# Grouped off-diagonal products, two late tile loads, and the merge weights' split on VectorE in a hybrid decoder layer

## The chip, the cores and the metric

The kernel runs on one core of one Trainium2 chip. Its time is the device time of a launch in microseconds (us). A core has TensorE (PE: matrix products, with PEld for its weight loads), VectorE (DVE), ScalarE (ACT), GpSimd (POOL) and SyncE (SP, which issues most DMAs). A profile is one execution taken by the hardware profiler; its clock column is the granted clock of TensorE, 1.00 for 2.4 GHz.

## The reference

One layer of a hybrid decoder, for a prompt of 1024 tokens (with 16 learned ones ahead of it) and 8 samples of 8 tokens, in float32 with 1024 model columns:

```
h = h + 1/2 * post1(SwiGLU_1(pre1(h)))                       # FFN 1, 2816 wide
u = pre_mix(h) @ w_in     # q|k|v (short conv), gate z, beta, decay, window q|k|v, two merge gates
A: gated DeltaNet, 8 heads of 128, chunks of 64, gated RMSNorm
B: attention over a window of 128 past tokens, 8 heads, sinks, ALiBi, 16 meta keys
y = sigmoid(gate_A) * o_A + sigmoid(gate_B) * o_B
h = h + post_mix(y @ w_out)                                  # the merge
h = h + 1/2 * post2(SwiGLU_2(pre2(h)))                       # FFN 2
```

Branch A, per head and chunk of 64 tokens:

```
a_mat = where(strict, beta * (k @ k.T) * decay, 0) + eye     # 64 x 64, lower triangular
u, w  = solve(a_mat, [v * beta | k * beta * exp(gc)])
step:  u' = u - w @ S;  o = (q * exp(gc)) @ S + (q @ k.T * decay) @ u'
       S  = S * c_decay + k_dec.T @ u'
```

Outputs are y for prompt and samples and the new states.

## The kernel before

Every large product is made from three products of parts: an operand is split into a high part (cast to a shorter format, names ending in h) and the rest (l), and hh + lh + hl is summed; L128, L130 and L132 are these three. FFN 1 runs first, then the projections and the window (branch B), then the eight heads of branch A, then the merge, then FFN 2. The order on PE is the order in which the program issues (manual); the instructions of the other engines are ordered by a scheduler, except where they are pinned to program order. `weave` interleaves several streams of work: each is given a begin and an end as shares of the whole, and a number of steps.

The heads (`heads`, 1273 to 1832 us). The 16 prompt tiles of 64 tokens are taken as eight chunks of 128 a head, in two halves g of four. A chunk needs the inverse R of its 128 x 128 triangular matrix: the two 64 x 64 diagonal inverses come by DMA (L1490), and the block off the diagonal is their product round a block bo. `prep` of a half makes it in two steps: L1502 multiplies bo by rt on the 64 x 64 tile of the array at (0, 64), ACT copies it out as xt (L1504), L1516 multiplies xt by R at (64, 0), and ACT copies the result into R (L1518). All use one PSUM buffer, tag "tr", as do the transposes for vs (L1510, scaled by ACT in L1512), the squares (L1539, ACT L1541, names sqp and cq) and the product of kf and q (L1527, DVE L1529, pm). `chain` carries the state S through the chunks: L1641, then DVE b (L1643), L1651 with R, ACT xs (L1653), L1656 and L1662, then DVE S (L1658) and o (L1664), ACT sq (L1602), DVE f (L1604), POOL f (L1606), ACT on (L1607). `emit` turns the outputs (L1689), multiplies them into the gate Z (L1691), adds the window's part yw (POOL, L1696) and stores y (L1697). Beside the chain of a head run the gate projection z of that head, the conv projections of the next, and the early part of the next head's preparation (`prep8`, then `prep` of the first half). Beside the gate of the last head `load_w` reads w_out, casts it (ACT, L1774) and subtracts (POOL, L1775) to get the low part, in 16 pieces of 128 x 512.

The merge (`run`, 1815 to 1945 us) takes nine tiles of tokens in the order 0, 4, 1, 5, 2, 8, 6, 3, 7. `load` of a tile reads y (L1877), casts its high part yh on ACT (L1791) and subtracts the low part yl on DVE (L1792). `tile_` makes 48 products a tile into two halves "dn", which ACT evacuates (L1900; L1897 for the short tile 8). `finish` norms it and adds the residual (L81, POOL L660, L82, L83, DVE L659, L90). `feed` turns an earlier tile (L207) and makes the operands of FFN 2 from it: ACT x10h to x70h (L213), DVE x10l to x70l (L214) and sums (L262 on DVE and POOL). Before, the load of the next tile is always issued ahead of the present tile's products.

Of the kernel before, what the change touches and what calls it, by code (L numbers as in the profile page):

```python
# [34 lines left out]
def f32(ap):  # L35
    return ap.bitcast(F32)
# [698 lines left out]
class Mixer:  # L735
# [733 lines left out]
    def persistent(self, pool):  # L1469
        c, nc = self.c, self.nc  # L1470
        self.ms = [c.t(pool, [P, 8, P], tag=f"ms{i}") for i in range(1)]
        self.p8 = [c.t(pool, [80, P], tag=f"p8{i}") for i in range(2)]
        self.on8 = c.t(pool, [P, 1, P], tag="on8")
        for m in (*self.ms, *self.p8, self.on8):
            nc.gpsimd.memset(m, 0.0)

    def prep(self, h, g, pool):

        c, nc = self.c, self.nc
        T = lambda shape, tag, bufs=None, dt=F32: c.t(pool, shape, dt, tag=tag, bufs=bufs)  # L1480
        x = self.hd[h]
        ts = range(4 * g, 4 * g + 4)
        cols = slice(4 * g * P, (4 * g + 4) * P)
        R = x["R", g] = T([P, 4, P], f"R{g}")
        rt = T([64, 4, 64], "rt", 2)
        bo = T([64, 4, 64], "bo", 2)
        nc.gpsimd.memset(R[64:P, :, 0:64], 0.0)
        for half in range(2):
            r = slice(half * 64, half * 64 + 64)
            nc.sync.dma_start(R[r, :, r], self.lr_d[h, ts.start:ts.stop, half].rearrange("t r c -> r t c"))  # L1490
        nc.sync.dma_start(rt, self.lrt_d[h, ts.start:ts.stop, 0].rearrange("t r c -> r t c"))
        nc.sync.dma_start(bo, self.bo_d[h][:, ts.start:ts.stop])
        kf = x["kf", g] = T([P, 4, P], f"kf{g}")
        nc.sync.dma_start(kf, self.kf_d[h][:, cols].rearrange("p (t k) -> p t k", k=P))
        pm = x["pm", g] = T([P, 4, P], f"pm{g}")
        nc.sync.dma_start(pm, self.dt_d[h][:, ts.start:ts.stop, :])
        kd = x["kd", g] = T([P, 4, P], f"kd{g}")
        nc.sync.dma_start(kd, self.kd_d[h][:, ts.start:ts.stop, :])

        px = self.ps([P, 4, P], "tr")  # L1500
        for t in range(4):
            nc.tensor.matmul(px[64:P, t, 0:64], bo[:, t, :], rt[:, t, :], start=True, stop=True, tile_position=(0, 64))  # L1502
        xt = T([P, 4, 64], "xt")
        nc.scalar.copy(xt[64:P], px[64:P, :, 0:64])  # L1504
        yield

        vs = x["vs", g] = T([P, 4, P], f"vs{g}")
        pt = self.ps([P, 4, P], "tr")
        for i, t in enumerate(ts):
            nc.tensor.transpose(pt[:, i, :], x["cv"][:, t * P:(t + 1) * P], self.k(C_IDENT))  # L1510
        for i, t in enumerate(ts):
            nc.scalar.activation(vs[:, i, :], pt[:, i, :], AF.Copy, scale=self.nr[:, h, t:t + 1])  # L1512
        yield
        px = self.ps([P, 4, P], "tr")
        for t in range(4):
            nc.tensor.matmul(px[0:64, t, 0:64], xt[64:P, t, :], R[64:P, t, 64:P], start=True, stop=True,  # L1516
                             tile_position=(64, 0))
        nc.scalar.copy(R[0:64, :, 64:P], px[0:64, :, 0:64])  # L1518
        yield

        cq = x["cq", g] = T([P, 4], f"cq{g}")
        self.squares(h, cq, [x["qv"][:, t * P:(t + 1) * P] for t in ts], pool)
        yield

        pk = self.ps([P, 4, P], "tr")
        for i, t in enumerate(ts):
            nc.tensor.matmul(pk[:, i, :], kf[:, i, :], x["qv"][:, t * P:(t + 1) * P], start=True, stop=True)  # L1527
        for i, t in enumerate(ts):
            nc.vector.scalar_tensor_tensor(out=pm[:, i, :], in0=pk[:, i, :], scalar=self.s[:, h, t:t + 1],  # L1529
                                           in1=pm[:, i, :], op0=ALU.mult, op1=ALU.mult)  # L1530
        yield
# [149 lines left out]
    def emit(self, h, pool):  # L1681

        nc = self.nc
        x = self.hd[h]
        Z = x["Z"]
        for on, t0, n, w in x["on"]:
            pt = self.ps([P, 4, P], "on")
            for i in range(n):
                nc.tensor.transpose(pt[:, i, :], on[:, i, :], self.k(C_IDENT))  # L1689
            zc = Z[:, t0 * P:t0 * P + n * w].rearrange("p (i w) -> p i w", w=w)  # L1690
            nc.vector.scalar_tensor_tensor(out=zc, in0=pt[:, :n, P - w:], scalar=self.nw, in1=zc, op0=ALU.mult,  # L1691
                                           op1=ALU.mult)
            cols = slice(t0 * P, t0 * P + n * w)
            yw = self.c.t(pool, [P, 512], tag="yw", bufs=1)
            nc.sync.dma_start(yw[:, :n * w], self.yw_d[h][:, cols])
            nc.gpsimd.tensor_tensor(out=Z[:, cols], in0=Z[:, cols], in1=yw[:, :n * w], op=ALU.add)  # L1696
            nc.sync.dma_start(self.y_d[t0][h], Z[:, cols])  # L1697
            yield

    def heads(self, pool, mg):  # L1700
        def early(h):
            yield from self.prep8(h, pool)
            yield from self.prep(h, 0, pool)

        def early0():
            prep = self.prep(0, 0, pool)
            yield from steps_of(prep, 1)
            yield from steps_of(prep8, 1)
            self.solves8(pool)
            yield from prep  # L1710
            yield from prep8

        z0 = self.z_gate(0, pool)
        prep8 = self.prep8(0, pool)
        weave((steps_of(z0, 72), 0, 1, 72), (early0(), 0.7, 1, 8))
        for h in range(H):
            streams = [(self.chain(h, pool), 0, 1, 29), (self.prep(h, 1, pool), 0, 0.35, 5)]
            if h:
                streams += [(self.emit(h - 1, pool), 0, 0.2, 3)]
            if h < H - 1:  # L1720
                if h:
                    streams += [(self.qv_steps(h + 1, pool), 0, 0.5, 145), (self.z_gate(h, pool), 0.5, 1, 145)]
                else:
                    streams += [(self.qv_steps(1, pool), 0, 0.55, 145), (z0, 0.55, 1, 73)]
                streams += [(early(h + 1), 0.75 if h else 0.8, 1, 8)]
            else:
                out = self.emit(h, pool)
                streams += [(self.z_gate(H - 1, pool, mg.load_w), 0, 0.95, 145), (steps_of(out, 2), 0.6, 1.15, 2)]
                begin = mg.begin()
                streams += [(steps_of(begin, 1), 0.6, 0.6, 1)]  # L1730
            weave(*streams)
        weave((begin, 0, 1, 42), (out, 0.1, 0.2, 1), (self.left, 0.15, 0.5, 4))
        drain(mg.begin_last(self.hd[H - 1]["Z"][:, 0:P]))
# [15 lines left out]
class Merge:  # L1749
# [8 lines left out]
    def load_w(self, i):  # L1758

        c, nc = self.c, self.nc  # L1760
        parts = new_chunk(c, self.xp[i], i)
        ks = ((2, 3, 4, 5), (6, 7), (0, 1))[i]
        flat, loaded = [x.rearrange("p k t -> p (k t)") for x in parts], []
        for j, k in enumerate(ks):
            wh, wl = (x[:, j * D:(j + 1) * D] for x in flat)
            raw = f32(c.t(self.m.wraw, [P, KD, P], F32R, tag="raw")).rearrange("p k f -> p (k f)")
            nc.sync.dma_start(raw, self.I["w_out"][:, k, :])
            self.w[k] = wh, wl
            loaded.append((raw, wh, wl))
        yield  # L1770
        for raw, wh, wl in loaded:
            for q in range(2):
                cols = slice(q * D // 2, (q + 1) * D // 2)
                c.tc.keep_in_program_order(nc.scalar.copy(wh[:, cols], raw[:, cols]))  # L1774
                nc.gpsimd.tensor_tensor(out=wl[:, cols], in0=raw[:, cols], in1=f32(wh[:, cols]), op=ALU.subtract)  # L1775
                yield

    def pair(self, yh, yl):
# [88 lines left out]
        yield from right(pool, self.f2.ptr, x8, y8, 8)  # L1867
        yield from right(pool, self.f2.ptr, self.o[3], self.o[7], 7)

    def load(self, t):  # L1870
        c, nc, pool = self.c, self.nc, self.pool
        n = min(TILES[t][1], 1088 - TILES[t][0])
        yl = c.t(pool, [P, H, P], F32R, tag="yl")
# [2 lines left out]
        for ks in (slice(0, H - 1), slice(H - 1, H)) if t == 4 else (slice(0, H),):  # L1876
            nc.sync.dma_start(f32(yl)[:, ks, :n], y[ks, :, t % 4 * P:t % 4 * P + n].rearrange("h p t -> p h t"))  # L1877
            if n == 64:
                self.pair(yh, yl)
            else:  # L1880
                self.split(yh, yl, ks, n)
        return yh, yl, n

    def tile_(self, t, yh, yl, n, o):
# [22 lines left out]
    def run(self, f2, es):  # L1907
# [9 lines left out]
        for i in range(1, 9):  # L1917
            if i == 5:
                f2.ahead(self.pool, "yl")
            now, y = y, self.load(order[i + 1]) if i < 8 else None  # L1920
            done = []
            if i > 1 and order[i - 2] != 6:

                done = [(self.feed(order[i - 2]), *((0.05, 0.45) if order[i - 2] in (4, 5) else (0.6, 0.95)), 2)]
            o = c.t(*((self.first, [P, H, P], F32R, "yh") if i % 3 == 0 else (self.pool, [P, H, P], F32R, "o")))
            weave((self.tile_(order[i], *now, f32(o).rearrange("p h t -> p (h t)")), 0, 1, 33 if order[i] == 8 else 49), *done)
        pso.close()


# [308 lines left out]
```

## Time and profile before

| | before |
|---|---|
| median of 3 runs | 2669.57 us (2669.01 to 2672.76) |
| profiled execution | 2665.62 us, span 2663.8 |
| mean granted clock | 0.992 |
| PE busy | 2593.7 us, 97% |
| DVE, ACT, POOL busy | 59%, 42%, 48% |
| chain that ended last | PE 47% |

Busy shares are means over stages with different limits: PE is full for most of the span, while the other engines have room, and only few stretches show PE idle. A wait in brackets behind a row of the timeline is idle time of that engine ahead of the row, with what ended it.

### The profile page before, as it was taken

To read this page: it belongs to the slowest core of one execution; us is meant where nothing else is said; L and a number is where in the kernel's file an instruction comes from. 1 tells how busy PE (TensorE), PEld (TensorE's weight loads), DVE (VectorE), ACT (ScalarE), POOL (GpSimd) and SP (SyncE) were. 2 spreads that over 40 slices of the span, in tenths; PEclk is the share of its full clock that TensorE was granted. 3 is DMA by queue.
4 is the path that set the end of the run, shared out by engine and by line. 5 is a ranking of instruction groups with operands and counts; after the bars stand their busy time and mean duration, and the time that the engine had idled before them with its cause. 6 is when DMAs were issued, how large, how long until landed. Compare 5 with 4: busy or idle time off the path is not lost.

```text
span 2663.8 us, 49377 instructions
## 1 busy us (share of the span) xinstructions
PE 2593.7 (97%) x18993; PEld 2475.1 (93%) x18993; DVE 1558.4 (59%) x2315; ACT 1130.7 (42%) x2728; POOL 1268.4 (48%) x1205
## 2 busy tenths in 40 slices
PE   7999999999999999999999999999899999999998
PEld 7999999999988999888889999997699999999998
DVE  7657565545677726995454444444466656554566
ACT  6333343432145634457444444454443434334221
POOL 6656555445524533433343333435565555554471
PEclk9999999999999999999999999999999999999999
DMA  4344343667544744335333333335443434338764
GB/s 164 121 152 152 127 167 117 242 227 253 190 151 151 230 148 130 106 122 176 98 106 88 89 95 99 100 93 160 138 132 140 167 127 149 127 137 319 244 225 145
DMA packets 231570, 406.48 MB, mean 153 GB/s; under 512 B 61814, under 2 KB 123414, under 8 KB 231046
## 3 DMA queue, kind: packets, MB, share of 16 engines
q1 hardware_dynamic: 211030, 324.75, 38.0%
q10 hardware_dynamic: 20304, 78.56, 7.5%
q8 instruction: 150, 2.46, 0.4%
q14 instruction: 86, 0.70, 0.1%
HBM read 264.36 MB, written 140.53 MB: 152 GB/s over the span
## 4 chain that ended last, share of the span: by engine, by line
PE 47%; DVE 1%; ACT 1%; POOL 1%; issue 1%; DMA 0%; POOLq 0%; DVEq 0%; SPq 0%; ACTq 0%
PE y L532 9%; PE B L352 7%; PE C L352 5%; PE A L352 4%; PE gu L132 4%; PE gu L128 4%; PE gu L130 4%; PE dn L128 1%; PE dn L132 1%; PE dn L130 1%; PE ch L1651 1%; PE tr L1527 1%; PE ch L1656 0%; PE oq L1646 0%; PE on L1673 0%
## 5 line engine op out<-in xcount | busy, mean ns | idle before, releaser
L132 PE MATMUL gu<-xh,wl 128*128 128x512 f32 (+3 forms) x1456 | 495.7, 340 | 0.0
L128 PE MATMUL gu<-xh,wh 128*128 128x512 f32 (+3 forms) x1456 | 491.9, 338 | 0.0
L130 PE MATMUL gu<-xl,wh 128*128 128x512 f32 (+3 forms) x1456 | 490.6, 337 | 0.0
L318 POOL TENSOR_TENSOR wl<-T,wh 128x512 fp32r<-128x512 f32 x246 | 330.5, 1350 | 314.1 <-ACT wh L317 244.4
L532 PE MATMUL y<-hb,wh 128*128 128x256 f32 (+2 forms) x2528 | 430.6, 290 | 2.1 <-ACT acc L572 1.0
L318 POOL TENSOR_TENSOR wl<-raw,wh 128x512 fp32r<-128x512 f32 x200 | 282.9, 1423 | 249.0 <-ACT wh L317 191.1
L532 PEld LDWEIGHTS y<-hb,wh 128*128 128x128 f32 x2528 | 366.1, 189 | 3.2 <-ACT acc L572 1.2
L317 ACT CAST wh<-T 128x512 fp32r<-128x512 f32 x246 | 152.2, 620 | 362.5 <-PE B L352 110.4
L132 PEld LDWEIGHTS gu<-xh,wl 128*128 128x128 f32 x1456 | 276.9, 190 | 16.4 <-issue 0.4
L130 PEld LDWEIGHTS gu<-xl,wh 128*128 128x128 f32 x1456 | 276.9, 190 | 16.3 <-issue 0.4
L128 PEld LDWEIGHTS gu<-xh,wh 128*128 128x128 f32 x1456 | 276.7, 190 | 16.4 <-issue 0.9
L532 PE MATMUL y<-hb,wl 128*128 128x256 f32 (+2 forms) x1264 | 271.8, 289 | 0.0
L317 ACT CAST wh<-raw 128x512 fp32r<-128x512 f32 x200 | 122.4, 621 | 276.8 <-PE C L352 81.9
L806 POOL TENSOR_TENSOR wl<-raw,wh 128x1024 fp32r<-128x1024 f32 x58 | 141.0, 2431 | 180.6 <-ACT wh L805 161.5
L543 DVE TENSOR_TENSOR acc<-acc,y 128x552 f32<-128x552 f32 (+4 forms) x216 | 144.9, 679 | 139.0 <-PE y L532 138.7
L532 PEld LDWEIGHTS y<-hb,wl 128*128 128x128 f32 x1264 | 207.1, 188 | 0.0
L292 DVE TENSOR_TENSOR T<-raw,raw 128x512 f32<-128x512 f32 x124 | 117.0, 948 | 107.1 <-POOL wl L318 107.1
L1606 POOL TENSOR_TENSOR f<-f,mhalf 128x1 f32<-128x1 f32 (+1 forms) x72 | 54.8, 762 | 125.5 <-DVE f L1604 119.2
L303 DVE TENSOR_TENSOR T<-raw,T 128x512 f32<-128x512 f32 x62 | 65.5, 1059 | 61.8 <-POOL wl L318 61.4
L292 DVE TENSOR_TENSOR T<-raw,T 128x512 f32<-128x512 f32 x62 | 63.3, 1028 | 31.9 <-POOL wl L318 31.5
L966 DVE SCALAR_TENSOR_TENSOR cv<-pc,cw,cv 128x1131 f32<-128x1131 f32 x48 | 66.8, 1393 | 21.4 <-POOL cv L963 20.8
L1111 DVE TENSOR_TENSOR ltmp<-la 72x14 f32<-72x14 f32 (+37 forms) x76 | 72.1, 948 | 12.3 <-DMA la<-b_d 11.4
(612 smaller groups left out, 7298.1 us busy)
## 6 DMA issues: line engine op xcount, KB each, us to landing
hb<-hid SPq DMA_DIRECT2D x71, 552.0 KB
hb<-hid SPq DMA_DIRECT2D x71, 544.0 KB
hid<-hs ACTq DMA_DIRECT2D x69, 552.0 KB
hid<-hs ACTq DMA_DIRECT2D x69, 544.0 KB
raw<-in_w_in_dram SPq DMA_DIRECT2D x58, 512.0 KB
raw<-in_ffn_w_gate_dram SPq DMA_DIRECT2D x100, 256.0 KB
raw<-in_ffn_w_up_dram SPq DMA_DIRECT2D x94, 256.0 KB
raw<-in_ffn_w_down_dram SPq DMA_DIRECT2D x88, 256.0 KB
```

The source lines that it names most:

```text
L128: nc.tensor.matmul(ps, wh, xh, start=first and i == 0, stop=False)
L130: nc.tensor.matmul(ps, wh, xl, start=False, stop=False)
L132: nc.tensor.matmul(ps, wl, xh, start=False, stop=last and i == n - 1)
L292: pin(self.nc.vector.tensor_tensor(out=b[name], in0=b[x], in1=b[y], op=ALU.subtract))
L317: self.nc.scalar.copy(hi, s)
L318: self.nc.gpsimd.tensor_tensor(out=lo, in0=s, in1=f32(hi), op=ALU.subtract)
L352: self.nc.tensor.matmul(self.view(ps, (i,)), w[a][:, k * P:(k + 1) * P], self.X[p][i][b][:, k, :], start=first and k + a + b == 0, stop=k ...
L532: self.nc.tensor.matmul(self.view(ps[d], (i,)), w[x][:, d * P:(d + 1) * P], hb[:, y, lo:hi], start=j + x + y == 0, stop=j == len(items) - ...
L543: dve = lambda out, x, y: nc.vector.tensor_tensor(out=out, in0=x, in1=y, op=ALU.add)
L806: low.tensor_tensor(out=lo, in0=raw, in1=f32(hi), op=ALU.subtract)
L966: nc.vector.scalar_tensor_tensor(out=cv, in0=pc[:, w:w + PADW], scalar=self.cw[:, j, w:w + 1], in1=cv, op0=ALU.mult, op1=ALU.add)
L1111: pin(nc.vector.tensor_tensor(out=t, in0=a[:n, 0:j, j:j + 1].to_broadcast([n, j, w]), in1=a[:n, j:j + 1, j + 1:size].to_broadcast([n, j, w ...
```

## The change

It has three parts.

1. Per head there is one group of small products on PE: the eight second products of this head, then the eight first products of the next, in one "tr" buffer of eight 64-column pieces. rt and bo are loaded as one DMA each, a head ahead; three R buffers are cleared once (`persistent`) instead of at every half. Head 0's first products come in a stream of their own, between 0.4 and 0.5 of the work ahead of head 0, which has 88 instead of 72 steps of the gate projection beside it, leaving 57 instead of 73 for head 0 itself.
2. The subtraction for w_out and the last head's Z add go from POOL to DVE.
3. While tiles 5 and 8 are multiplied (i of 3 and 5), the load, cast and split of the next tile (2 and 6) are issued at 0.45 of the products instead of ahead of them, with cast and split pinned to program order.

```
+    def inverses(self, h, pool):
+        x, nc = self.hd[h], self.nc
+        for g in range(2):
+            R = x["R", g] = self.R[g + g * (h % 2)]
+            for half in range(2):
+                r = slice(half * 64, half * 64 + 64)
+                nc.sync.dma_start(R[r, :, r], self.lr_d[h, 4 * g:4 * g + 4, half].rearrange("t r c -> r t c"))
+        if 0 < h < H - 1:
+            self.off_load(h + 1, pool)
+
+    def first_products(self, h, px, pool):
+        rt, bo = self.off
+        for t in range(8):
+            self.nc.tensor.matmul(px[64:P, t], bo[:, t], rt[:, t], start=True, stop=True, tile_position=(0, 64))
+        self.xt[h] = self.c.t(pool, [P, 8, 64], tag="xt")
+        self.nc.scalar.copy(self.xt[h][64:P], px[64:P])
+
+    def second_products(self, h, px):
+        xt = self.xt.pop(h)
+        for t in range(8):
+            self.nc.tensor.matmul(px[0:64, t], xt[64:P, t], self.hd[h]["R", t // 4][64:P, t % 4, 64:P], start=True,
+                                  stop=True, tile_position=(64, 0))
+
+    def blocks_out(self, h, px):
+        for g in range(2):
+            self.nc.scalar.copy(self.hd[h]["R", g][0:64, :, 64:P], px[0:64, 4 * g:4 * g + 4])
...
 def prep(self, h, g, pool):
-        nc.gpsimd.memset(R[64:P, :, 0:64], 0.0)
...
+        if h and not g:
+            self.inverses(h, pool)
...
-        px = self.ps([P, 4, P], "tr")
-        for t in range(4):
-            nc.tensor.matmul(px[64:P, t, 0:64], bo[:, t, :], rt[:, t, :], start=True, stop=True, tile_position=(0, 64))
-        xt = T([P, 4, 64], "xt")
-        nc.scalar.copy(xt[64:P], px[64:P, :, 0:64])
-        yield
+        if not g:
+            px = self.ps([P, 8, 64], "tr")
+            self.second_products(h, px)
+            if h < H - 1:
+                self.first_products(h + 1, px, pool)
+            self.blocks_out(h, px)
+            yield
...
+        self.off_load(0, pool)
+        self.inverses(0, pool)
+        weave((steps_of(z0, 88), 0, 1, 88), (off0(), 0.4, 0.5, 1), (early0(), 0.7, 1, 7))
...
-                nc.gpsimd.tensor_tensor(out=wl[:, cols], in0=raw[:, cols], in1=f32(wh[:, cols]), op=ALU.subtract)
+                nc.vector.tensor_tensor(out=wl[:, cols], in0=raw[:, cols], in1=f32(wh[:, cols]), op=ALU.subtract)
...
+            late = i in (3, 5)
+            now, y = y, self.load(order[i + 1]) if i < 8 and not late else None
+            def load_next():
+                got.append(self.load(order[i + 1], c.tc.keep_in_program_order))
+                yield
...
+                  *([(load_next(), 0.45, 0.45, 1)] if late else []))
```

PE in head 2, first half (gu are the gate projection's products, ch and oq the chain's). Before, the first products stand alone, and the second products (L1516) come 24 rows further on, and both again in the second half:

```order
L130 MATMUL gu_16830<-xl_1327_8949,wh_16739 128x256
L1502 MATMUL tr_16857<-rt_16844,bo_16845 64x64 x4
L132 MATMUL gu_16830<-xh_1326_8948,wl_16740 128x256
...
L130 MATMUL gu_16915<-xl_1329_8954,wh_16739 128x320
L1516 MATMUL tr_16918<-R_2818_16843,xt_16862 64x64 x4
L132 MATMUL gu_16915<-xh_1328_8953,wl_16740 128x320
```

After, on PE in the same place of the program, second products (now L1507) and the next head's first (L1500) stand together:

```order
L128 MATMUL gu_16813<-xh_1326_8948,wh_16734 128x256
L1507 MATMUL tr_16857<-R_2436_15264,xt_16107 64x64 x4
L1507 MATMUL tr_16857<-R_2437_15265,xt_16107 64x64 x4
L1500 MATMUL tr_16857<-rt_16847,bo_16848 64x64 x8
L130 MATMUL gu_16813<-xl_1327_8949,wh_16734 128x256
L1680 MATMUL ch_16879<-xs_16832,kd_2667_16239 128x128
```

The pairs of groups of both halves have become one group; the rows of the second half have none.

DVE while tile 8 is multiplied (sums and x70l to x30l are FFN 2's operands, yl_22220 and yl_22166 are tile 6). Before:

```order
L1792 TENSOR_TENSOR yl_22220<-yl_22220,yh_22221 128x1024
L262 TENSOR_TENSOR sum_22233<-tr_22234,sum_22232 128x512
L214 TENSOR_TENSOR x70l_21805<-sum_22232,x70h_21804 128x4x128
L214 TENSOR_TENSOR x60l_21790<-sum_22233,x60h_21789 128x4x128
L214 TENSOR_TENSOR x50l_21795<-o_21931,x50h_21794 128x4x128
L214 TENSOR_TENSOR x30l_21775<-o_21931,x30h_21774 128x4x128
L90 SCALAR_TENSOR_TENSOR o_22117<-o_22117,rn_22195,g_ffn_norm_pre_21847 128x1024
```

After, on DVE at the same place:

```order
L262 TENSOR_TENSOR sum_22131<-tr_22132,sum_22130 128x512
L214 TENSOR_TENSOR x70l_21708<-sum_22130,x70h_21707 128x4x128
L214 TENSOR_TENSOR x60l_21693<-sum_22131,x60h_21692 128x4x128
L214 TENSOR_TENSOR x50l_21698<-o_21834,x50h_21697 128x4x128
L214 TENSOR_TENSOR x30l_21678<-o_21834,x30h_21677 128x4x128
L90 SCALAR_TENSOR_TENSOR o_22020<-o_22020,rn_22098,g_ffn_norm_pre_21750 128x1024
L1824 TENSOR_TENSOR yl_22166<-yl_22166,yh_22167 128x1024
```

The split (L1792, now L1824) has moved from ahead of the second sum to behind L90. On ACT the cast (now L1823) has moved in the same way, from ahead of x70h to between x30h and the evacuation of tile 8 (now L1929).

DVE near the end of the last head, where the chain's S, o, b and f stand. Before:

```order
L1658 SCALAR_TENSOR_TENSOR S_21561<-S_21509,cdec_9693,ch_21559 128x128
L1664 TENSOR_TENSOR o_21565<-oq_21563,qs_21532 128x128
L1431 SCALAR_TENSOR_TENSOR Z_21094<-tz_21577,gu_21495 128x256
L1643 SCALAR_TENSOR_TENSOR b_21589<-ch_21587,ne_1441_9691,vs_3875_21194 128x128
L1604 SCALAR_TENSOR_TENSOR f_21569<-so_21111,cq_3899_21280 128x1
```

After, on DVE at the same place (S is now L1682, o L1688, b L1667, f L1628; xl is the low part of w_out):

```order
L1807 TENSOR_TENSOR xl_3894_21389<-raw_21390,xh_3893_21388 128x512
L1720 TENSOR_TENSOR Z_21018<-Z_21018,yw_21447 128x64
L1682 SCALAR_TENSOR_TENSOR S_21464<-S_21412,cdec_9693,ch_21462 128x128
L1807 TENSOR_TENSOR xl_3894_21389<-raw_21390,xh_3893_21388 128x512
L1688 TENSOR_TENSOR o_21468<-oq_21466,qs_21435 128x128
L1431 SCALAR_TENSOR_TENSOR Z_21018<-tz_21480,gu_21398 128x256
L1667 SCALAR_TENSOR_TENSOR b_21492<-ch_21490,ne_1441_9691,vs_3808_21071 128x128
L1807 TENSOR_TENSOR xl_3894_21389<-raw_21392,xh_3893_21388 128x512
L1628 SCALAR_TENSOR_TENSOR f_21472<-so_21035,cq_3829_21151 128x1
```

Two of the subtractions (L1807) have come directly ahead of o and f here, one ahead of the Z add (L1720) and of S; in the whole head sixteen subtractions and three Z adds have come between the chain's rows.

## Rows read from the trace of the kernel before

**Rows 1.** The page, part 1: busy time, share of the span, instructions per engine.

```profile
PE 2593.7 (97%) x18993; PEld 2475.1 (93%) x18993; DVE 1558.4 (59%) x2315; ACT 1130.7 (42%) x2728; POOL 1268.4 (48%) x1205
```

**Rows 2.** Windows: window, length, busy PE, PEld, DVE, ACT, POOL, granted clock, DMA, GB/s.

```profile
1600.00:1660.00 60.00, 59.99 (x415) 54.72 (x414) 26.43 (x58) 27.65 (x96) 24.88 (x28) 1.00 0.37 106
1890.00:1910.00 20.00, 11.66 (x40) 9.00 (x39) 12.94 (x10) 8.22 (x13) 10.04 (x9) 0.74 0.33 105
```

**Rows 3.** Waits of PE, 1270 to 1960 us: total, times, longest.

```profile
PE dn L128 <- ACT o L1897: 8.3, 1, 8.3
PE tr L1527 <- ACT sqp L1541: 2.1, 2, 1.4
...
PE dn L128 <- ACT yh L1900: 1.5, 1, 1.5
```

**Rows 4.** Timeline of PE round one group of small products: start, length, operation.

```profile
1412.04 0.28 PE L130 MATMUL gu<-xl,wh 128*128 128x256 f32 x1
1412.25 0.67 PE L1502 MATMUL tr<-rt,bo 64*64 64x64 f32 x8
1412.85 0.39 PE L132 MATMUL gu<-xh,wl 128*128 128x256 f32 x1
1413.08 0.28 PE L128 MATMUL gu<-xh,wh 128*128 128x256 f32 x1
...
1413.55 0.28 PE L130 MATMUL gu<-xl,wh 128*128 128x256 f32 x1
```

**Rows 5.** The small products by source line: ns min/median/max, first and last start.

```profile
L1502 PE MATMUL tr<-rt,bo x128: 218/219/268, 1281.1 to 1775.1; 64*64 64x64 f32 x128
...
L1516 PE MATMUL tr<-R,xt x128: 217/218/268, 1285.0 to 1782.2; 64*64 64x64 f32 x128
```

**Rows 6.** Groups of ACT, 1270 to 1785 us: busy, mean ns; idle before.

```profile
L1518 ACT COPY R<-tr 64x256 f32<-64x256 f32 x16 | 5.9, 366 | 10.7 <-PE tr L1516 10.7
```

**Rows 7.** Timeline of PE after tile 8's last product.

```profile
1900.08 0.79 PE L128 MATMUL dn<-xh,yh 128*128 128x512 f32 x1 [8.34 <-ACT o L1897]
...
1901.10 0.63 PE L132 MATMUL dn<-xh,yl 128*128 128x512 f32 x1
...
1905.37 0.51 PE L128 MATMUL dn<-xh,yh 128*128 128x512 f32 x1
```

**Rows 8.** Timeline of ACT in the same stretch.

```profile
1889.89 1.05 ACT L1791 CAST yh<-yl 128x1024 fp32r<-128x1024 f32 x1 [1.43 <-DMA yl<-y_d]
...
1894.61 0.62 ACT L213 CAST x60h<-sum 128x512 fp32r<-128x512 f32 x1 [3.15 <-DVE sum L262]
...
1898.01 0.62 ACT L213 CAST x30h<-o 128x512 fp32r<-128x512 f32 x1 [1.05 <-POOL o L262]
1899.44 1.07 ACT L1897 COPY o<-dn 128x512 f32<-128x512 f32 x2 [0.81 <-DVE x30l L214]
```

**Rows 9.** Timeline of DVE in the same stretch.

```profile
1890.97 3.00 DVE L1792 TENSOR_TENSOR yl<-yl,yh 128x1024 fp32r<-128x1024 f32 x1 [2.43 <-ACT yh L1791]
1893.90 0.68 DVE L262 TENSOR_TENSOR sum<-tr,sum 128x512 f32<-128x512 f32 x1
...
1899.80 1.28 DVE L90 SCALAR_TENSOR_TENSOR o<-o,rn,g_ffn_norm_pre 128x1024 f32<-128x1024 f32 x1 [0.44 <-POOL rn L83]
```

**Rows 10.** Timeline of POOL in the same stretch.

```profile
1890.53 2.36 POOL L660 TENSOR_TENSOR o<-o,res 128x1024 f32<-128x1024 f32 x1
1894.72 3.26 POOL L262 TENSOR_TENSOR o<-o,sum 128x512 f32<-128x512 f32 x2 [1.83 <-DVE sum L262]
```

**Rows 11.** Timeline of DVE at the change from tile 5 to tile 2.

```profile
1862.15 1.23 DVE L1792 TENSOR_TENSOR yl<-yl,yh 128x1024 fp32r<-128x1024 f32 x1
```

**Rows 12.** Timeline of DVE near the end of the last head.

```profile
1813.61 0.35 DVE L1643 SCALAR_TENSOR_TENSOR b<-ch,ne,vs 128x128 f32<-128x128 f32 x1 [0.45 <-PE ch L1641]
1814.37 1.14 DVE L1604 SCALAR_TENSOR_TENSOR f<-so,cq 128x1 f32<-128x1 f32 x1 [0.42 <-POOL xl L1775]
```

**Rows 13.** Timeline of PE near the end of the last head.

```profile
1814.22 0.38 PE L1651 MATMUL ch<-b,R 128*128 128x128 f32 x2
```

More of the change, by code (lines that the diff above doesn't have):

```diff
@@ L1473, in persistent, with off_load @@
         self.on8 = c.t(pool, [P, 1, P], tag="on8")
-        for m in (*self.ms, *self.p8, self.on8):
+        self.R = [c.t(pool, [P, 4, P], tag=f"R{i}") for i in range(3)]
+        self.xt = {}
+        for m in (*self.ms, *self.p8, self.on8, *self.R):
             nc.gpsimd.memset(m, 0.0)
+    def inverses(self, h, pool):
[7 more added lines that the diff above has]
+            self.off_load(h + 1, pool)
+    def off_load(self, h, pool):
+        rt, bo = (self.c.t(pool, [64, 8, 64], tag=tag) for tag in ("rt", "bo"))
+        self.nc.sync.dma_start(rt, self.lrt_d[h, :, 0].rearrange("t r c -> r t c"))
+        self.nc.sync.dma_start(bo, self.bo_d[h])
+        self.off = rt, bo
+    def first_products(self, h, px, pool):
[12 more added lines that the diff above has]
+            self.nc.scalar.copy(self.hd[h]["R", g][0:64, :, 64:P], px[0:64, 4 * g:4 * g + 4])
     def prep(self, h, g, pool):
@@ L1483, in prep @@
         cols = slice(4 * g * P, (4 * g + 4) * P)
-        R = x["R", g] = T([P, 4, P], f"R{g}")
-        rt = T([64, 4, 64], "rt", 2)
-        bo = T([64, 4, 64], "bo", 2)
-        nc.gpsimd.memset(R[64:P, :, 0:64], 0.0)
[L1488 to L1492, printed above, removed]
+        if h and not g:
+            self.inverses(h, pool)
         kf = x["kf", g] = T([P, 4, P], f"kf{g}")
@@ L1512, in prep @@
             nc.scalar.activation(vs[:, i, :], pt[:, i, :], AF.Copy, scale=self.nr[:, h, t:t + 1])
[L1513 to L1518, printed above, removed]
         yield
@@ L1695, in emit @@
             nc.sync.dma_start(yw[:, :n * w], self.yw_d[h][:, cols])
-            nc.gpsimd.tensor_tensor(out=Z[:, cols], in0=Z[:, cols], in1=yw[:, :n * w], op=ALU.add)
+            (nc.vector if h == H - 1 else nc.gpsimd).tensor_tensor(out=Z[:, cols], in0=Z[:, cols], in1=yw[:, :n * w],
+                                                                   op=ALU.add)
             nc.sync.dma_start(self.y_d[t0][h], Z[:, cols])
@@ L1703, in early, with off0 @@
             yield from self.prep(h, 0, pool)
+        def off0():
+            self.first_products(0, self.ps([P, 8, 64], "tr"), pool)
+            self.off_load(1, pool)
+            yield
         def early0():
             prep = self.prep(0, 0, pool)
-            yield from steps_of(prep, 1)
             yield from steps_of(prep8, 1)
@@ L1714, in heads @@
         prep8 = self.prep8(0, pool)
-        weave((steps_of(z0, 72), 0, 1, 72), (early0(), 0.7, 1, 8))
+        self.off_load(0, pool)
+        self.inverses(0, pool)
+        weave((steps_of(z0, 88), 0, 1, 88), (off0(), 0.4, 0.5, 1), (early0(), 0.7, 1, 7))
         for h in range(H):
-            streams = [(self.chain(h, pool), 0, 1, 29), (self.prep(h, 1, pool), 0, 0.35, 5)]
+            streams = [(self.chain(h, pool), 0, 1, 29), (self.prep(h, 1, pool), 0, 0.35, 3)]
             if h:
@@ L1723, in heads @@
                 else:
-                    streams += [(self.qv_steps(1, pool), 0, 0.55, 145), (z0, 0.55, 1, 73)]
-                streams += [(early(h + 1), 0.75 if h else 0.8, 1, 8)]
+                    streams += [(self.qv_steps(1, pool), 0, 0.55, 145), (z0, 0.55, 1, 57)]
+                streams += [(early(h + 1), 0.75 if h else 0.8, 1, 7)]
             else:
@@ L1868, in rest, with load @@
         yield from right(pool, self.f2.ptr, self.o[3], self.o[7], 7)
-    def load(self, t):
+    def load(self, t, pin=lambda op: op):
         c, nc, pool = self.c, self.nc, self.pool
@@ L1880, in load @@
             else:
-                self.split(yh, yl, ks, n)
+                self.split(yh, yl, ks, n, pin)
         return yh, yl, n
@@ L1919, in run @@
                 f2.ahead(self.pool, "yl")
-            now, y = y, self.load(order[i + 1]) if i < 8 else None
-            done = []
+            late = i in (3, 5)
+            now, y = y, self.load(order[i + 1]) if i < 8 and not late else None
+            done, got = [], []
+            def load_next():
+                got.append(self.load(order[i + 1], c.tc.keep_in_program_order))
+                yield
             if i > 1 and order[i - 2] != 6:
@@ L1925, in run @@
             o = c.t(*((self.first, [P, H, P], F32R, "yh") if i % 3 == 0 else (self.pool, [P, H, P], F32R, "o")))
-            weave((self.tile_(order[i], *now, f32(o).rearrange("p h t -> p (h t)")), 0, 1, 33 if order[i] == 8 else 49), *done)
+            weave((self.tile_(order[i], *now, f32(o).rearrange("p h t -> p (h t)")), 0, 1, 33 if order[i] == 8 else 49), *done,
+                  *([(load_next(), 0.45, 0.45, 1)] if late else []))
+            y = got[0] if late else y
         pso.close()
```

## The prediction

> **What bounds the kernel now.** I read the page first, then windows over the heads and the merge, then PE's waits, then timelines. The page has PE busy for 97% of the span [rows 1], but that mean hides two kinds of place. In the heads PE has no slack: 59.99 of 60 us busy, clock 1.00, while DVE, ACT and POOL stand near 25 us each [rows 2]. There only less work on PE shortens the kernel, and a microsecond of PE saved is a microsecond gained as long as no wait grows in its place. Between tiles of the merge PE is short of work: one wait of 8.34 us, for ACT's evacuation L1897, is the longest of the stretch [rows 3, 7], and in the window round it PE is busy 11.66 of 20 us at a mean clock of 0.74 [rows 2]. So the grouping has to be priced in PE time in the heads, and the late load by what ends last before that one wait.
>
> The durations come from the profiled execution, which took 2665.62 us (span 2663.8); the median of the runs is 2669.57, 3.95 us more. I sum against the execution and add the 3.95 at the end.
>
> **Grouping the small products.** Before, the products of L1502 and L1516 come in 32 groups of eight passes: 128 passes from each line [rows 5], which in the order are groups of four products at two passes each. One such group is seen whole at 1412.25 [rows 4]. Ordinary 256-column products follow each other at 0.1175 us (1413.08 to 1413.55 holds four intervals). From the start of the product before the group to the start of the second product behind it is 1412.04 to 1413.08, 1.04 us, and two ordinary intervals would be 0.235: the group costs 0.805 us. Of that eight passes are eight times 0.058 = 0.46 (they start inside 0.46 us, the first interval about 0.05 longer than the others); the other 0.34 is paid for entering and leaving: a late start, a gap of 0.15 behind the last pass, and 0.11 that the second product behind comes late.
>
> After, the number of passes is the same, 256, but in nine groups: one of eight products ahead of the heads, seven of sixteen, one of eight for head 7. So 32 - 9 = 23 entries and exits go: 23 x 0.34 = 7.8 us. Inside each of the seven large groups the position of the tile in the array changes once. If that costs what a first interval costs, 7 x 0.05 = 0.4 comes off: 7.4 us, which I take, since the only thing the rows show of a start inside the small mode is that first interval. If each change costs a full entry and exit, there are in effect 16 groups and the gain is 16 x 0.34 = 5.4.
>
> The row at 1412.85 shows that PE pays on leaving the small products. The Trainium skill ("TensorEngine Tiling (Array Packing)", Key Properties) says that a change of tiling mode drains the engine while a change of tile within a mode does not. By that rule the sum is the 7.8 to 7.4 of nine groups, not the 5.4 of sixteen; no row of before shows two positions side by side.
>
> What else the grouping moves. Each head has one ACT block behind its group: two copies of 0.366 into R [rows 6] and one of 512 columns into xt, which I estimate at under 0.73 by doubling that row, so 1.46 us in all, on an engine busy 27.65 of 60 us [rows 2]. The bank "tr" is held that long, and PE's next user of it, the transposes for vs, comes several products behind the group; I cost the wait at nothing, and at 7 x 1.05 = 7.4 us if the cover fails, 1.05 being the mean of the two waits that users of that bank had on ACT in the prologue and head 0 (2.1 us, [rows 3]). rt and bo are loaded a whole head ahead of use, some 66 us (15 steps of half a head from 1281.1 to 1775.1, [rows 5]), and have one buffer each; before, they had two and were loaded close to use. 16 memsets on POOL and 16 DMA issues on SP go; neither engine is waited for there. In the prologue the 16 further z products lie beside the waits for sqp (2.1 us, [rows 3]), but head 0 has 16 fewer to put beside its chain, and SP now lets the loads of kd, r, kf and pm wait behind head 1's rt, which waits for PE's first products. Bounds: -1.5 (most of the 2.1 covered) and +1.5 (the same wait again); I take 0.
>
> **The late load.** Before, at tile 8, ACT's cast L1791 for tile 6 waits for its DMA and ends 1890.94, DVE's split L1792 behind it takes 3.00 us beside POOL's L660 (2.36), and everything that empties the transposed tiles stands behind it: sum L262 at 1893.90, x60h on ACT (which waited 3.15 for it), POOL's L262, x30h, and only then the evacuation at 1899.44 [rows 8 to 10]. Alone the same split takes 1.23 [rows 11]. In the changed order the cast stands behind x30h, the split behind L90. The second sum can then follow x40l at about 1889.7, 4.2 us earlier. But L660 is not moved: it starts at 1890.53 and lasts 1.8 to 2.4, so POOL's two L262 run from about 1892.5 to 1895.1 (two at 1.3; they took 3.26 under contention, [rows 10]). Then x30h 0.6, cast 1.05, first evacuation 0.6: PE resumes at about 1897.4 instead of 1900.08, gain 2.7. The third product needs yl: x30l, L90 1.28 [rows 9], split 1.23 put it at about 1899.1 against 1901.10 [rows 7], gain 2.0. The later wait counts: 2.0. The clock: before, products run 0.427 apart from 1901.10 to 1905.37 (10 intervals, [rows 7]) where 0.235 is full rate, so 13 of them cost 2.5 us. The idle time shrinks but stays, so I leave that cost in. Bounds: 0.5 (L262 as slow as before) to 9.7 (idle time down to the evacuation's own 1.2, and full rate).
>
> At the change from tile 5 to tile 2 the wait was 1.53 [rows 3], and there the split took only 1.23 [rows 11]. It too is put behind L90, so the third product, not the first, becomes late: resume about 1 us earlier, split about 1 us later than PE would like. I take 0, bounds -0.6 and +0.9.
>
> **Weights split on DVE.** The 16 subtractions leave POOL, where one of them held up f (0.42 us, then 1.14 for an operation on one column, [rows 12]); DVE does them in about 0.62 each (half of 1.23, [rows 11]). Most stand where DVE idles. Behind them in the order are b, S and o of the last head's chain. b ended 1813.96 and PE used it at 1814.22 [rows 12, 13]: 0.26 us of slack. Two links of the chain get a split or two directly ahead of o and b and lose about 0.4 to 0.7 each; the contention that goes gives about 1 us back. The last head's Z add moves too and is stored earlier, but the merge's copies L1859 stand ahead of the next split on DVE and wait for PE, so nothing is gained. Sum 0, bounds -2 (no link is late) and +8 (13 splits of 0.62 ahead of a chain step).
>
> **Sum.** 7.4 + 0 + 2.0 + 0 + 0 = 9.4: the execution becomes 2656.2, the median 2660.2; I say 2660.
>
> **Rivals.**
> *The stall at tile 8 goes almost whole.* The split of 3.00 was the head of the queue; if POOL's L660 also shrinks and PE keeps its full clock, the merge gives 9.7 instead of 2.0: 2669.6 - 7.4 - 9.7 = 2652.5. For it: one releaser for the whole 8.34. Against it: L660 and two L262 stand in POOL's queue in either order.
> *The grouping is paid back in waits.* If PE finds the "tr" bank taken behind each large group, 7.4 us come back: 2669.6 - 7.4 + 7.4 - 2.0 = 2667.6. For it: a group holds the bank twice as long as before. Against it: several products and chain steps lie between, and ACT is under half busy.
> *Slower: DVE sets the last head's pace.* If splits reach DVE's queue as casts finish late, each stands between two chain steps: 13 x 0.62 = 8.1, three Z adds of about 0.68 (a 512-column sum, [rows 9]) make 2.0, and a half-rate stretch like that of [rows 7] adds 2.5: 12.6 against the 9.4, 2672.8. It decides from 0.26 us on, the slack of b; the forecast already spends about 1 us of it, which the lost contention repays. Against it: DVE is busy 26 of 60 us.
>
> **How the numbers follow.** Forecast 0.57 (own range 2656 to 2664, from the 5.4 and the bounds of the merge), stall gone 0.15, paid back 0.18, DVE's pace 0.10. Within 0.2% is 5.3 us either way, about what a measurement of this kernel can tell from no change. Faster by more: 0.52 of the forecast's 0.57, 0.15 and 0.04 of the third, 0.71. Slower by more needs the last rival and a smaller grouping as well: 0.05. The rest, 0.24, is no change. The range, 2653 to 2668, leaves out the end of the first rival and most of the last.
>
> **What would show it.** Right: nine groups of the small products, with a step between positions near 0.1 us; windows of the heads full as before and about 0.9 us earlier per head; the wait before tile 6 near 6 us, and one of about 1 us two products later, for yl. Wrong: a PE wait for "tr" after each group; a group start inside the group; PE waiting for b or S from 1794 to 1816 us by more than 1 us in all; or the wait before tile 6 below 3 us.

## The result, and the profile after

| | before | after |
|---|---|---|
| median of 20 runs | 2668.97 us (2662.06 to 2673.22) | 2674.07 us (2667.31 to 2677.11) |
| ratio, 95% interval | | 1.0018 [1.0012, 1.0024] |
| profiled execution's span | 2663.8 us | 2672.6 us |
| PE busy | 2593.7 us | 2587.0 us |

The forecast was 2660 and a gain; the kernel became 5.1 us slower. PE is busy 6.7 us less in a span that is 8.8 us longer, so the loss is waiting. Windows (window, length, busy PE, PEld, DVE, ACT, POOL, granted clock, DMA share, GB/s), first one of the kernel before that [rows 2] has not:

```profile
1290.00:1360.00 70.00, 66.28 (x455) 59.30 (x455) 31.95 (x68) 34.60 (x116) 24.93 (x34) 1.00 0.31 85
```

Then those of the kernel after:

```profile
1290.00:1360.00 70.00, 60.16 (x394) 53.78 (x393) 26.13 (x58) 32.15 (x111) 18.45 (x27) 0.93 0.34 94
1350.00:1360.00 10.00, 8.42 (x53) 7.93 (x54) 2.23 (x5) 3.63 (x12) 0.92 (x3) 0.54 0.16 41
1600.00:1660.00 60.00, 59.40 (x432) 55.43 (x431) 27.55 (x58) 29.98 (x99) 20.91 (x27) 1.00 0.33 97
1890.00:1910.00 20.00, 12.80 (x51) 9.58 (x50) 13.07 (x12) 9.36 (x17) 11.42 (x9) 0.85 0.43 132
```

From 1290 to 1360 us lie the end of the stretch ahead of head 0 (the prologue) and most of head 0. PE is without a product there for 9.8 us, where it was 3.7 before, and from 1350 to 1360 its clock is near half. A middle head (1600 to 1660) is no longer quite full: 0.6 us idle. The merge's window is a little better than before; the same stretch comes about 7 us later in this trace, and from 1897 to 1917 PE is busy 12.80 us too, at 0.83. PE's waits of the kernel after (total, times, longest), where [rows 3] stood before:

```profile
PE dn L128 <- ACT o L1929: 6.3, 1, 6.3
PE tr L1507 <- ACT vs L1611: 3.6, 6, 0.6
PE tr L1610 <- POOL v L979: 3.4, 1, 3.4
PE A L352 <- ACT g L384: 2.7, 1, 2.7
PE dn L132 <- DVE yl L1824: 2.7, 3, 0.9
PE tr L1551 <- ACT sqp L1565: 2.6, 2, 1.8
PE gu L132 <- POOL wl L806: 1.7, 1, 1.7
...
PE gu L128 <- ACT wh L805: 1.0, 1, 1.0
```

Three of them are new and in no part of the prediction's sum: wl and wh, v, and vs (L1611). The wait for g, at the start of FFN 2, was 1.2 before.

Where the time went, with the first product of a place in both traces set against each other: the heads begin 1.6 us later in the trace of after. From there up to the first step of head 1's chain 10.4 us are lost (1364.06 before, 1376.00 after). Heads 1 to 7 win back 3.1 (to 1813.18 and 1821.97), the stretch into the merge 1.9 (to 1832.68 and 1839.56), and the merge 1.1 (to FFN 2's first product, 1938.26 and 1944.00). In the first stretch of FFN 2, to the last product of x10h into C (1960.6 and 1969.7), 3.4 are lost, with the wait for g in it. One trace places such sums only to a few us, since executions of one kernel differ by some 10 us; the medians below decide.

The waits in head 0, first as PE sees them (start, length, operation, idle time before and what ended it):

```profile
1316.33 0.50 PE L128 MATMUL gu<-xh,wh 128*128 128x512 f32 x1 [0.98 <-ACT wh L805]
...
1318.76 0.50 PE L132 MATMUL gu<-xh,wl 128*128 128x512 f32 x1 [1.70 <-POOL wl L806]
```

```profile
1351.58 0.43 PE L1610 MATMUL tr<-ident,v 128*80 128x128 f32 x1 [3.45 <-POOL v L979]
```

Then ACT's cast of the same weight, for the convolution of v:

```profile
1315.23 1.04 ACT L805 CAST wh<-raw 128x1024 fp32r<-128x1024 f32 x1 [0.20 <-PE gu L130]
```

The cast starts only when PE has finished the last product with another weight, and PE then stands until the cast and, behind it, POOL's subtraction (2.35 us) are through. The order in the program shows why. Weights wh and wl have two buffers. Before, the gate's first weight is used up in 72 steps (24 times three products) ahead of head 0, and its second is loaded in head 0, behind the two convolutions. With 88 steps the second weight is loaded and begun ahead of head 0 and not finished before the convolutions are through: it holds one buffer, and the convolutions' weights take turns in the other.

### The profile page after: what moved, and what is told of

Same layout as the page of the kernel before. It is cut to its first block, busy times and chain, and to the rows that moved or that the text cites. A ratio compares the mean times of both kernels' runs of the same rounds, so it can differ in the third digit from the quotient of the medians.

```text
span 2672.6 us, 49307 instructions
## 1 busy us (share of the span) xinstructions
PE 2587.0 (97%) x18993; PEld 2472.0 (92%) x18993; DVE 1564.8 (59%) x2334; ACT 1128.4 (42%) x2720; POOL 1240.5 (46%) x1173
## 5 line engine op out<-in xcount | busy, mean ns | idle before, releaser
L805 ACT CAST wh<-raw 128x1024 fp32r<-128x1024 f32 x60 | 62.8, 1046 | 42.5 <-PE gu L130 42.4
```

## The experiments

Each was timed beside the kernel before. The ratios are those of the runs side by side.

| kernel | median us | ratio to before, 95% interval |
|---|---|---|
| after | 2674.07 | 1.0018 [1.0012, 1.0024] |
| e1_z72: after, division 72 and 73 | 2663.90 | 0.9980 [0.9970, 0.9989] |
| e2_group: grouping alone, 88 and 57 | 2679.29 | 1.0045 [1.0033, 1.0058] |
| e3_late: before and the late loads | 2668.11 | 0.9998 [0.9988, 1.0008] |
| e4_dve: before and the DVE part | 2667.01 | 0.9995 [0.9987, 1.0004] |
| e5_z88: before, division 88 and 57 | 2675.70 | 1.0030 [1.0019, 1.0041] |
| e6_vs: e1_z72, vs ahead of the copies | 2660.03 | 0.9969 [0.9958, 0.9979] |
| e7_vs_nolate: e6_vs, no late loads | 2662.77 | 0.9983 [0.9974, 0.9992] |
| e8_alt: e1_z72, positions in turn | 2660.21 | 0.9972 [0.9961, 0.9983] |
| e9_vs_alt: e6_vs and e8_alt | 2652.14 | 0.9937 [0.9924, 0.9949] |
| e10_z76: before, division 76 and 69 | 2680.56 | 1.0041 [1.0029, 1.0054] |
| e11_pro: e9_vs_alt, prologue earlier | 2653.02 | 0.9940 [0.9928, 0.9952] |

**The division of the gate projection put back (e1_z72).**

```
-        weave((steps_of(z0, 88), 0, 1, 88), (off0(), 0.4, 0.5, 1), (early0(), 0.7, 1, 7))
+        weave((steps_of(z0, 72), 0, 1, 72), (off0(), 0.4, 0.5, 1), (early0(), 0.7, 1, 7))
...
-                    ... (z0, 0.55, 1, 57)]
+                    ... (z0, 0.55, 1, 73)]
```

> The changed kernel with one thing put back: the gate projection of head 0 is again divided 72 steps ahead of head 0 and 73 in it, instead of 88 and 57. Theory A (the division is what costs): the 16 products of the gate's second weight done early hold one of the two weight buffers through head 0's convolutions and shorten the cover ahead of v. Then the waits for wh and wl (2.7 us in all), the wait for v (3.4) and the half-rate stretch of 10.2 us in head 0 go, and the kernel takes 8 to 9 us less than the changed one: 2665 to 2666. Theory B (the large group and its one buffer cost head 0 the time): head 0 stays as late, 2672 to 2674.

2663.90, 10.2 us less than after, 1 to 2 us more than theory A said; B falls. The largest waits of PE from 1285 to 1375 us are now those of the prologue and of chain links, and none for wh, wl or v is left. All waits there sum to 6.3 us, against 12.1 in the kernel after:

```profile
PE tr L1551 <- ACT sqp L1565: 1.8, 2, 1.3
PE ch L1680 <- ACT xs L1677: 1.5, 1, 1.5
PE tr L1601 <- ACT sqp L1565: 0.9, 1, 0.9
```

One part of theory A did not come true: the half-rate clock did not go. This trace has a lower clock in two places, without the waits for wh, wl and v:

```profile
1290.00:1300.00 10.00, 8.95 (x42) 7.95 (x43) 2.20 (x8) 4.82 (x16) 2.47 (x2) 0.66 0.64 182
1350.00:1360.00 10.00, 9.47 (x61) 8.99 (x59) 1.54 (x6) 6.26 (x22) 0.20 (x1) 0.71 0.37 97
```

Over all runs the mean granted clock is 0.9903 in the kernel after and 0.9909 here. That difference is worth about 1.6 us of 2670 (an estimate from these two numbers), so the clock is the smaller part of the 10.2 us; PE's waits from 1285 to 1375 in these two traces differ by 5.8 us. Nor does all of it lie in head 0: the first stretch of FFN 2, with the wait for g, takes 25.7 us in the kernel after and 22.4 here (22.3 before), about 3 us that the theory does not speak of.

**The division alone (e5_z88)**, on the kernel before, without any grouping: 72 to 88 and 73 to 57 in the same two lines.

> The kernel before with one thing changed: the gate projection of head 0 is divided 88 steps ahead of head 0 and 57 in it (72 and 73 before). Theory A (the division alone brings the loss, whatever the grouping): a wait for wh and wl near 2.7 us and one for v near 3.4 appear in head 0, and the kernel takes 6 to 10 us more: 2675 to 2679. Theory B (the loss needs the large group and its buffer): within 2 us of before, 2667 to 2671.

2675.70: 8.1 us more than the 2667.64 beside it. The same three waits as in the kernel after appear in PE's waits of head 0, though no large group is there:

```profile
PE tr L1586 <- POOL v L979: 2.9, 1, 2.9
...
PE gu L132 <- POOL wl L806: 1.7, 1, 1.7
PE gu L128 <- ACT wh L805: 1.4, 1, 1.4
```

So the grouping has no part in them. The clock from 1350 to 1360 us is 0.83 in this trace, where it was 0.54 in the kernel after: much the same waits did not bring the same loss of clock.

**Buffer or cover (e10_z76).** Only four products of the second weight go early (76 and 69).

> The kernel before with the gate projection of head 0 divided 76 and 69: only four products of the second weight are done early. Theory A1 (what costs is the weight buffer that the second weight holds from then on): nearly all of the loss of the 88 and 57 division stays, 2673 to 2676, and the waits for wh and wl in head 0 are near 2.7 us. Theory A2 (what costs is the cover that head 0 loses, 16 products of about 0.2 us): a quarter of it, 2669 to 2670, and no wait for wh or wl.

2680.56, not a quarter of the loss but more than all of it. PE's waits in head 0, and the clock in two windows:

```profile
PE gu L132 <- POOL wl L806: 1.7, 1, 1.7
...
PE gu L128 <- ACT wh L805: 1.4, 1, 1.4
```

```profile
1288.00:1303.00 15.00, 12.82 (x52) 10.76 (x52) 1.97 (x7) 5.62 (x20) 2.38 (x1) 0.54 0.51 141
1322.00:1330.00 8.00, 6.43 (x22) 5.56 (x23) 3.38 (x5) 0.81 (x3) 4.70 (x5) 0.57 0.19 67
```

The waits for the weight are whole with four products early: they belong to the buffer. The wait for v is gone, which fits the cover (the products that PE has to do in the meantime): 12 of the 16 products are back in head 0, and 12 times the 0.235 us of a product at full rate are 2.8 us, against a wait of 2.9 in e5_z88.

The time fits neither theory. The two windows are at half rate for about 21 of their 23 us. The five runs have a mean granted clock of 0.9874, those of the kernel before beside them 0.9909; the difference is worth about 9 of the 12.1 us (an estimate from these numbers), so the clock, and not the waits' own 3.1 us, is most of this kernel's loss. But the longer stretch, 1288 to 1303, lies ahead of the waits for the weight, which end at 1321.14 and 1323.57: it follows the waits of the prologue, which came out longer here than in either neighbour. Why they did stays open. So this run shows whose the waits are, and not what the buffer costs by itself.

**vs ahead of the masked copies (e6_vs).** In the kernel after, the group L1507 waits 0.6 us a head. PE, then ACT in front of it:

```profile
1424.61 0.97 PE L1507 MATMUL tr<-R,xt 64*64 64x64 f32 x13 [0.59 <-ACT vs L1611]
1425.37 0.27 PE L1500 MATMUL tr<-rt,bo 64*64 64x64 f32 x1
1425.42 0.22 PE L1507 MATMUL tr<-R,xt 64*64 64x64 f32 x1
...
1425.59 0.92 PE L1500 MATMUL tr<-rt,bo 64*64 64x64 f32 x13
1426.44 0.39 PE L130 MATMUL gu<-xl,wh 128*128 128x256 f32 x1
```

```profile
1422.25 0.60 ACT L1430 ACTIVATE tz<-gu 128x512 f32<-128x512 f32 x1 [0.90 <-PE gu L132]
1422.74 1.56 ACT L1584 ACTIVATE kds<-kd,smask 80x128 f32<-80x128 f32 x5
1424.21 0.35 ACT L1611 ACTIVATE vs<-tr,nr__1447_9701 80x128 f32<-80x128 f32 x1
```

vs empties the bank that the group wants, and five copies that nobody waits for stand ahead of it on ACT. They stood there before, too, but the gate's tz came behind vs, and vs was done ahead of the first products at 1412.25 ([rows 4]):

```profile
1410.17 1.56 ACT L1560 ACTIVATE kds<-kd,smask 80x128 f32<-80x128 f32 x5
1411.63 0.35 ACT L1587 ACTIVATE vs<-tr,nr__1447_9701 80x128 f32<-80x128 f32 x1
1411.88 0.58 ACT L1430 ACTIVATE tz<-gu 128x512 f32<-128x512 f32 x1
```

In the kernel after, ACT idles 0.90 us for tz first, and the copies and vs start only behind it. So the wait takes both, tz ahead and the copies ahead; the run changes the second.

```
-        masked(range(4, 9))
         ...
-        nc.scalar.activation(vs[:80], pt[:80, 0, :], AF.Copy, scale=self.nr[:80, h, 8:9])
+        c.tc.keep_in_program_order(nc.scalar.activation(vs[:80], pt[:80, 0, :], AF.Copy, scale=self.nr[:80, h, 8:9]))
+        masked(range(4, 9))
```

> The changed kernel with 72 and 73 steps, and in the preparation of the samples (prep8) ACT's scaling of vs ahead of the last five masked copies kds, not behind them. Theory: PE's group waits 0.6 us a head for vs only because five copies of 0.31 us stand ahead of it on ACT; then the seven waits go, 4 us less than with 72 and 73 steps alone: 2660. Rival (the bank is simply held too long by the transpose and its copy): no change, 2664.

2660.03, 3.9 us less than e1_z72. ACT and PE at the same place (the line of vs is L1610 here):

```profile
1412.06 0.35 ACT L1610 ACTIVATE vs<-tr,nr__1447_9701 80x128 f32<-80x128 f32 x1
1412.31 1.56 ACT L1584 ACTIVATE kds<-kd,smask 80x128 f32<-80x128 f32 x5
```

```profile
1413.05 0.28 PE L128 MATMUL gu<-xh,wh 128*128 128x256 f32 x1
1413.26 0.97 PE L1507 MATMUL tr<-R,xt 64*64 64x64 f32 x13
```

The group no longer waits in heads 1 to 7, though tz still stands ahead of vs (1411.56). The window from 1600 to 1660 us is full again (59.99 of 60 us).

**Positions in turn (e8_alt).**

```
+        for t in range(8):
+            self.nc.tensor.matmul(px[0:64, t], xt[64:P, t], ..., tile_position=(64, 0))
+            if h < H - 1:
+                rt, bo = self.off
+                self.nc.tensor.matmul(px[64:P, t], bo[:, t], rt[:, t], ..., tile_position=(0, 64))
```

> The changed kernel with 72 and 73 steps, and the sixteen products of a group issued in turn: one of this head at array position (64, 0), one of the next head at (0, 64), and so on. If a change of position costs what an entry costs (0.34 us): 14 more changes a head, 4.8 us a head, 33 us more, 2697. If it costs a first interval (0.05 us): 0.7 us a head, 2669. If the two positions work beside each other: the passes come at half the interval, 0.8 us less a head, 2658. If only the order of issue counts: 2664.

2660.21, 3.7 us less than e1_z72, so a change of position inside the group costs nothing; it gains, though less than the 0.8 us a head that would give 2658. PE in one group (L1511 is here the product at (0, 64)):

```profile
1414.55 0.27 PE L1507 MATMUL tr<-R,xt 64*64 64x64 f32 x1 [0.60 <-ACT vs L1621]
1414.65 0.24 PE L1511 MATMUL tr<-rt,bo 64*64 64x64 f32 x1
1414.66 0.28 PE L1507 MATMUL tr<-R,xt 64*64 64x64 f32 x2
...
1415.49 0.28 PE L1511 MATMUL tr<-rt,bo 64*64 64x64 f32 x2
1415.70 0.39 PE L130 MATMUL gu<-xl,wh 128*128 128x256 f32 x1
```

From the first pass to the next ordinary product 1.15 us, where the group in the kernel after takes 1426.44 - 1424.61 = 1.83. Each position keeps its pace of about 0.059 us a pass, and the two run beside each other. The Trainium skill ("TensorEngine Tiling (Array Packing)", Key Properties) says that different tiles can work in parallel; the rows agree, 32 passes in 1.15 us against 1.83.

**The parts at the merge (e3_late, e4_dve, e2_group, e7_vs_nolate).** e3_late adds only `late`, `load_next` and the pins to the kernel before; e4_dve only the two changes from gpsimd to vector; e2_group is the kernel after without both; e7_vs_nolate is e6_vs with `late = False`.

> The kernel before with the two late loads alone. Reading of the traces: the wait before tile 6 shrinks by about 2 us but a wait for the split follows it, net 0.9 won; tile 2 loses 0.2; and FFN 2's first products wait about 2.8 us longer (half-rate clock included), since in the later tiles an ACT copy now stands ahead of an evacuation. Sum +2: 2671. As predicted (-2.0): 2667.

> The kernel before with the merge weights' split and the last head's Z add on DVE alone. Reading of the traces: the stretch from the last head into the merge is 1.6 us shorter: 2667.4. As predicted (0): 2669. If DVE sets the pace of the last head's chain: 2672.

> Grouping alone: the changed kernel without the two late loads and with the merge weights' split and the last Z add back on POOL; the division 88 and 57 is kept. Theory A: head 0 loses about 10 us and heads 1 to 7 win back 3, so 2674 to 2676. Theory C (the loss comes from the parts at the merge): 2668 or less.

> As the kernel with vs ahead of the masked copies, but without the two late loads. If the late loads lose at FFN 2's start what they win before tile 6: within 1 us of that kernel. If they win their 2 us, as predicted: 2 us more than it. If they only move time: 1 to 2 us less.

Alone, on the kernel before, neither can be told from no change (-0.6 and -1.7 us, both intervals hold 1); my reading that the late loads lose 2 us was wrong. Taking the late loads out of e6_vs costs 2.7 us in the medians, with intervals that overlap; that is close to the 2.0 of the forecast, but from another place, as the waits below show. Together the two parts were worth more in the kernel after: e2_group is 5.2 us above it. At 2679.29 e2_group lies above even theory A's range, and C falls. Its five runs have a lower mean clock (0.9888 against 0.9903), about 4 us by the same estimate, so not all of the 5.2 is the two parts' own work. PE's waits at the merge show the tile changes of e2_group and of e7_vs_nolate, in this order:

```profile
PE dn L128 <- ACT o L1928: 7.4, 1, 7.4
PE dn L128 <- ACT yh L1931: 3.0, 1, 3.0
PE A L352 <- ACT g L384: 2.7, 1, 2.7
PE dn L128 <- ACT yh L1822: 1.9, 1, 1.9
```

```profile
PE dn L128 <- ACT o L1929: 7.4, 1, 7.4
PE dn L128 <- ACT yh L1932: 3.0, 1, 3.0
```

With the late loads, in e6_vs, the first two are 6.3 and 0.6, with 2.7 in three waits for yl beside them, of which 0.8, at the first tile, is there without them as well. So at tile 6 they save 0.1 us of waiting (7.35 against 6.28 and 0.94), and at tile 2 1.5 us (3.02 against 0.58 and 0.92); behind the 3.02 PE's products also follow each other at 0.43 us, half rate. The forecast had its 2.0 at tile 6 and 0 at tile 2. The wait at tile 2 is 1.5 in the kernel before ([rows 3]) and in e10_z76, but 3.0 in e5_z88, which groups nothing, as in e2_group and e7_vs_nolate; what sets it is not shown. The wait for g at FFN 2's start is 2.7 in the kernel after and in e2_group and 1.2 in the others; what makes it longer there is not shown. The division alone does not, since e5_z88 has 1.2.

**Both gains together (e9_vs_alt), and the prologue (e11_pro)**, which differs by one line, `(off0(), 0.35, 0.35, 1), (early0(), 0.55, 1, 7)`.

> The two improvements together on 72 and 73 steps: vs ahead of the masked copies, and the sixteen products of a group issued in turn between the two array positions. If they add up (3.9 and 3.7 us less than 72 and 73 steps alone): 2656 to 2657. If the wait taken away hides the shorter group: 2660.

> The kernel with both improvements, and in the stretch ahead of head 0 the first products at 0.35 and the early preparation from 0.55 on (0.4 to 0.5 and 0.7 before). If more products beside its chain of waits cover them (0.7, 0.4, 1.2 and 0.8 us with vs ahead of the masked copies): up to 2 us less than with both improvements. If the loads of rt, R and r set the pace there: the same or up to 2 us more.

2652.14 is the fastest version, 0.63% [0.51%, 0.76%] under before; the two gains add up and somewhat more (11.8 us under e1_z72, 7.6 expected, within what medians of six runs can differ by). The earlier prologue starts head 0 about 2 us sooner in its trace, counted from where the heads begin. The median, 2653.02, does not show it: no difference.

## Why the prediction was wrong, point by point

- *The prologue and head 0: 0, bounds -1.5 to +1.5.* This is the step that failed. Medians put the division of the gate projection at +10.2 (after less e1_z72; by the traces some 3 of it lie at the start of FFN 2), and on the kernel before, alone, at +8.1. I priced the 16 products as cover that moves from one place to another, and did not ask which buffer they hold: the second weight keeps one of two from then on. The cover was under-priced as well: head 0's wait for v, 3.4 us, is a wait that did not exist before, so my bound, "the same wait again" for the ones that [rows 3] show, could not hold it. Behind the wait for v the clock also fell, to 0.54 from 1350 to 1360, and I had reckoned with half rate only at the merge; by the mean clocks of the runs that is the smaller part of the loss.
- *"tr": no wait behind the group.* Behind it there is one, of 0.6 us, in the prologue (L1540 for ACT's copy R), and none in heads 1 to 7. The wait came ahead of the group, for vs, 3.6 us in six heads; taking it away won 3.9. The rival looked at the wrong side of the group and priced a wait at 1.05, nearly twice what it was (7.4 for seven). Before, the first products followed vs too ([rows 4]), but ACT did tz behind vs, so that vs was done in time.
- *Nine groups, 7.4 us.* Right in mechanism and near in size. In e6_vs the trace gains 6.8 us from the first chain step of head 1 to that of head 7, 1.1 a head, where 7.4 over eight heads are 0.9. No group start is paid inside the group: where the position changes the passes run on (1425.37 to 1425.59 in the rows above). That the passes could be made to overlap, as in e8_alt, was not in the sum.
- *Late load at tile 8: 2.0.* Mechanism right, size too large. The first product is freed 2.1 us earlier (6.26 against 8.34, [rows 7]), then the third waits 0.94 for yl:

```profile
1905.15 0.80 PE L128 MATMUL dn<-xh,yh 128*128 128x512 f32 x1 [6.26 <-ACT o L1929]
...
1907.31 0.80 PE L132 MATMUL dn<-xh,yl 128*128 128x512 f32 x1 [0.94 <-DVE yl L1824]
```

  I had put the first product 2.7 us earlier and the third 2.0. The third comes 2.16 us behind the first where it was 1.02 ([rows 7]), so it gains 0.9. L660 took 2.80 on POOL, not 1.8 to 2.4, with DVE's x60l beside it (2.84 us); no run separates the two. So POOL's queue, which the forecast named as the reason why the stall would stay, stayed. The two rows of DVE and POOL, answering to [rows 9, 10]:

```profile
1897.82 2.84 DVE L214 TENSOR_TENSOR x60l<-sum,x60h 128x512 fp32r<-128x512 f32 x1
```

```profile
1897.31 2.80 POOL L660 TENSOR_TENSOR o<-o,res 128x1024 f32<-128x1024 f32 x1
```

- *Weights on DVE: 0, bounds -2 to +8.* -1.7 alone, inside the bounds and not to be told from 0. DVE did not become the bound of the last head.
- *Sum.* With the two unpriced waits mended (e6_vs) the kernel takes 2660.03, the forecast's 2660. That agreement is luck: it rests on terms that are each off by one or two us, in a kernel with another division and another order on ACT than the one that was forecast.

## What to carry to other kernels

When work is moved earlier to fill a hole, ask not only what it covers but what it holds: the first product with a new weight takes a buffer until the last one. Here, with two buffers, a weight left half used made the casts of the other weights wait for PE. Cut such a stream at the end of a weight. And a bank with one buffer has to be priced on both sides: what empties it ahead of its next user may stand behind work of that engine that nobody waits for.

## What the runs showed of the hardware

- Products of 64 x 64 at array positions (64, 0) and (0, 64), issued in turn into the same PSUM buffer but different partitions, run beside each other: 32 passes in 1.15 us, against 1.83 when sixteen passes of one position are followed by sixteen of the other.
- A few waits of 1 to 3.5 us close together could bring the granted clock down: 0.54 from 1350 to 1360 us in the kernel after and 0.54 from 1288 to 1303 in e10_z76, where the clock cost more than the waits. They did not always: the same place was at 0.83 in e5_z88, and from 1314 to 1322 us the kernel after kept 1.00 through the waits for wh and wl, behind which e10_z76 was at 0.57.
